# Score products on half the rows, the bias table loaded by each mixer, and a kernel's first two weight pairs in one sweep

## The chip, the cores and the metric

The kernel runs on one core of one Trainium2 chip. The metric is the time of one execution on the device, in microseconds (us), as the median of several runs. In the profile PE is the matrix engine (PEld its weight loads, which run beside the products), DVE the vector engine, ACT the scalar engine, POOL the general one, SP the engine that issues most transfers. Every engine works through its own list of instructions in order and waits on semaphores for the others.

## The reference

Two layers of a Conformer-like trunk on an input of 512 tokens by 1024 features, in fp32. Cut to what matters:

```python
for l in range(2):
    x = x + 0.5 * swiglu(rms_norm(x, ffn1_norm[l]), ...)       # 1024 -> 2816 -> 1024
    h = rms_norm(x, mix_norm[l])
    a, g, q, k, v = split(h @ w_in[l])                          # 512 columns each
    conv_out = conv_module(a, g, ...)                           # GLU, 31 causal taps, norm, swish
    # q, k: 4 heads x 2 maps x 64 features, each normed over its 64 features
    # v: 4 heads x 128 features; 128 queries at a time, causal
    s = q . k / sqrt(64) + bias[bucket(distance)]               # for each head and each of 2 maps
    p = softmax(s)
    attn = rms_norm((p[map 0] - lam * p[map 1]) @ v) * (1 - lambda_init)
    x = x + concat(conv_out, attn) @ w_out[l]
    x = x + 0.5 * swiglu(rms_norm(x, ffn2_norm[l]), ...)
```

The point for this study is the score: for each head there are two maps, and each contracts over 64 features only, whereas the array of PE has 128 rows.

## The kernel before, in words

Activations are kept with features on the partitions: `x` is 8 tiles of 128 features by 512 tokens. Every large fp32 product is made of three cheaper ones in a format that PE reads in one pass: an operand is split into a rounded part `hi` and a remainder `lo`, and `mm3` (L162, L165, L166) adds hi x hi, hi x lo and lo x hi. For a weight chunk of 128 by 1024, `chunk` (L104) issues the load on SP's queue, ACT makes `whi` (L96), DVE or POOL makes `wlo` (L97). The chunks live in rings of 5 raw, 4 `whi` and 4 `wlo` buffers, so a load waits until an older chunk has been used. An activation tile gets the same treatment in `Prep.tile`: ACT rounds `x` times the norm's gain into `acth` (L247), DVE makes `actl` (L248), ACT squares the tile (L252, L255) and POOL adds the squares. The root mean square of a token is only applied after the products: `rows_rstd` sums the squares over features with four PE transposes (L206) and DVE, `spread` puts the result on all partitions by two PE products (L230), and ACT copies it to `rb` (L234).

A feed-forward block has 22 pairs of a gate and an up chunk, in groups of 6, 8 and 8. The six of the first group are plain products with one PSUM bank for each of gate and up (three pairs of banks in rotation: pair 3 takes the banks of pair 0). The other 16 go through `seven` (L352), a seven-product scheme on half-size blocks. After the last pair of a group, its down products follow. For the very first block, the first pair's weight chunks are loaded ahead, in halves of four feature tiles (`lead`, `cuts=2`), between the first tile of `x` and the others. `first_products` multiplies pair 0 with feature tiles as the outer loop, gate and up as the inner one, and then pair 1, one bank after the other. The results are read by DVE with `rb` (L420, L422), gated, and split into `hh` and `hl` (L391, L392).

The mixer projects convolution inputs, keys, queries and values. The queries are transposed to features on the partitions (`to_features`, L598) and copied by ACT into `qz` (L605), which has a copy for each map; in the copy of map 0 the features of map 1 are zero, since the scale `gq` is zero there, and the reverse. So a score product contracts over all 128 rows, and the zeros take the other map out. A head's two score products (L677) are fp32 and go to one bank of tag `sc` and one of tag `po`; each is two PE instructions in the trace. DVE adds the bias table and takes the extreme value of a row (L681), ACT takes the exponential (L685), DVE combines both maps. `keys_first` transposes the combined map on PE (L698) and `values` multiplies it with the values (L707). `attend(n)` sets the scores of step n beside the transposes of step n-2 and the values of n-3, for 16 steps (4 blocks of queries, last one first, by 4 heads; the blocks have 512, 384, 256 and 128 keys). Beside this run the 31 taps of the convolution, on DVE, POOL and ACT (`conv_taps`), and the products of the value projection (L589 to L591) and, later, of the output projection (`ps_out`).

The bias table, 128 by 4 by 512, is made once: a small product with 33 rows (L459) looks up the buckets, two small DRAM tiles hold the result, and a load on POOL's queue with a skewed address pattern fills the tile `bias`, which stays in on-chip memory to the end. The parameter columns of layer 0 are loaded on ACT's queue, those of layer 1 on POOL's.

The order on each engine is fixed when the program is built: a scheduler simulates engines and queues with its own model and writes each engine's list. So a change of data flow can also change the order of products that the source does not touch. Ahead of the change's places, that order sets what can start when.

Of the kernel before, what the change touches and what calls it, by code (L numbers as in the profile page):

```python
# [11 lines left out]
F32 = mybir.dt.float32  # L12
# [3 lines left out]
ALU = mybir.AluOpType  # L16
# [50 lines left out]
def trunk(ctx: ExitStack, tc: tile.TileContext, xt, par, lamv, relb, onehot,  # L67
# [28 lines left out]
        S.activation(hi, raw, AF.Copy)  # L96
        (eng or V).tensor_tensor(out=lo, in0=raw, in1=f32(hi), op=ALU.subtract)  # L97

    def chunk(src, eng=None, cuts=1):
        raw, hi, lo = ring("wraw"), ring("whi"), ring("wlo")  # L100
        n = 1024 // cuts
        for c in range(cuts):
            s = slice(c * n, (c + 1) * n)
            nc.sync.dma_start(raw[:, s], src[:, s])  # L104
            parts_of(raw[:, s], hi[:, s], lo[:, s], eng)
        return hi, lo

    def gather(src, blocks, eng=None):
# [65 lines left out]
    for l in range(DEPTH):  # L174
        pt = const.tile([P, NPAR], F32, tag=f"par{l}", name=f"par{l}")
        pars.append(pt)
    nc.scalar.dma_start(pars[0], par[0])
    nc.sync.dma_start(x[:, 0, :], xt[0])
    lead = [chunk(gu1[0, 0, i], cuts=2) for i in range(2)]
    for k in range(1, KT):  # L180
        nc.sync.dma_start(x[:, k, :], xt[k])
    nc.gpsimd.dma_start(pars[1], par[1])
    ident = const.tile([P, P], F32, tag="ident", name="ident")
    make_identity(nc, ident)
    ones = const.tile([P, P], F32, tag="ones", name="ones")
# [75 lines left out]
    def wpart(w, b, n=P):  # L261
        return w[0][:, b * n : (b + 1) * n], w[1][:, b * n : (b + 1) * n]

    def products(pr, w, ps, i, pin=False):
        for k in range(KT):
            mm3(ps, wpart(w[i], k), pr[k], k == 0, k == KT - 1, pin=pin and k == 0)

    def first_products(pr, w, ps, early=False):

# [112 lines left out]
    def ffn(pr, gu, dn, after, lead=None, aside=None):  # L382
        with tc.tile_pool(name="ffn", bufs=1) as fp:
            r = halves = None
            for m0, many in PARTS:
                hh, held, late = [], [], []

                def gated(n, us):
                    hi = fp.tile([P, SEQ], F32R, tag=f"hh{n}", name="hh")
                    lo = fp.tile([P, SEQ], F32R, tag=f"hl{n}", name="hl")  # L390
                    S.activation(hi, us, AF.Copy)  # L391
                    V.tensor_tensor(lo, us, f32(hi), op=ALU.subtract)  # L392
                    hh.append((hi, lo))

                def finish():
                    if late:
                        n, rest = late.pop()
                        gated(n, rest())

                for mm in range(many):  # L400
                    m = m0 + mm
                    if m == 4 and aside:
                        aside()
                    if m >= PLAIN:
                        w = sums(gu[m, 0], gu[m, 1])
                        late.append((mm, seven(halves, w, pair_banks(m), fp, finish, mm == many - 1)))
                        continue
                    w = lead if lead and m == 0 else [chunk(gu[m, 0]), chunk(gu[m, 1])]
                    held.append((mm, w, pair_banks(m)))
                    if m == 0:  # L410
                        continue
                    if m == 1:
                        _, _, r = first_products(pr, [h[1] for h in held], [h[2] for h in held])
                    else:
                        for i in range(2):
                            products(pr, w, held[-1][2][i], i)
                    for n, _, ps in held:
                        gs = fp.tile([P, 2, SEQ], F32, tag="gn", name="gs", bufs=2)
                        us = gs[:, 1]
                        V.tensor_tensor(gs[:, 0], ps[0], r, op=ALU.mult)  # L420
                        S.activation(gs[:, 0], gs[:, 0], AF.Silu)
                        V.tensor_tensor(us, ps[1], r, op=ALU.mult)  # L422
                        V.tensor_tensor(us, us, gs[:, 0], op=ALU.mult)
                        gated(n, us)
                    held = []
                    if m == 1:
                        halves = Halves(fp, pr, r)
                finish()
                if m0 == 0:
                    halves.settle()  # L430
                blocks = [divmod(m0 + kk, HALF) for kk in range(many)]
                blocks = [(half, m * HALF + f) for m in range(KT) for half, f in blocks]
                w = None
                for m in range(KT):

                    ps = bank(turn_tag(m0 + many + m // 2), "ps_d")
                    for kk in range(many):
                        b = m * many + kk
                        if b % 8 == 0:
                            w = gather(dn, blocks[b : b + 8])  # L440
                        mm3(ps, wpart(w, b % 8), hh[kk], kk == 0, kk == many - 1)
                    V.scalar_tensor_tensor(x[:, m, :], ps, 0.5, x[:, m, :], op0=ALU.mult, op1=ALU.add)  # L442
                    if m0 + many == FT:
                        after(m)


    bias = const.tile([P, HEADS, SEQ], F32, tag="bias", name="bias")

    def make_bias():
        ext = small.tile([NBUCKET + 1, HEADS], F32, tag="relb", name="relb", bufs=1)  # L450
        V.memset(ext, MASK)
        nc.gpsimd.dma_start(ext[:NBUCKET, :], relb)
        d1 = dram.tile([HEADS, RLEN], F32, tag="d1", name="d1")
        for a, n in ((0, 512), (512, RLEN - 512)):
            oh = tmp.tile([P, SEQ], F32, tag="sq", name="oneh")[: NBUCKET + 1, :n]
            nc.gpsimd.dma_start(oh, onehot[:, a : a + n])
            row = tmp.tile([P, SEQ], F32, tag="sq", name="brow")[:HEADS, :n]
            ps = bank("tp", "ps_bias")
            T.matmul(ps[:HEADS, :n], ext, oh, start=True, stop=True)  # L459
            V.tensor_scalar(row, ps[:HEADS, :n], -1.0, None, op0=ALU.mult)  # L460
            nc.gpsimd.dma_start(d1[:, a : a + n], row)
        d2 = dram.tile([HEADS, P, RLEN], F32, tag="d2", name="d2")
        nc.gpsimd.dma_start(d2, d1.unsqueeze(1).broadcast_to([HEADS, P, RLEN]))
        skew = bass.AP(d2.tensor, d2.offset + P - 1, [[RLEN - 1, P], [P * RLEN, HEADS], [1, SEQ]])
        nc.gpsimd.dma_start(bias, skew)


    nlam, gq, gsub, ghalf = [], [], [], []
# [1 line left out]
    def make_scalars():  # L470
        for l in range(DEPTH):
# [9 lines left out]
            nl = const.tile([P, 1], F32, tag=f"nlam{l}", name=f"nlam{l}")  # L481
            V.scalar_tensor_tensor(nl, e[:, 1:2], -lambda_init(l), e[:, 0:1], op0=ALU.add, op1=ALU.subtract)
            nlam.append(nl)
            g = const.tile([P, 2], F32, tag=f"gq{l}", name=f"gq{l}")
            V.memset(g, 0.0)
            for m in range(2):
                d = slice(m * HD, (m + 1) * HD)
                V.scalar_tensor_tensor(
                    g[d, m : m + 1], col(l, "q_norm")[d], -math.sqrt(HD), col(l, "k_norm")[d],
                    op0=ALU.mult, op1=ALU.mult,  # L490
                )
# [12 lines left out]
    def mixer(l, pr, after):  # L504
        with tc.tile_pool(name="mix", bufs=1) as mp, tc.tile_pool(name="mt", bufs=2) as mt:
# [34 lines left out]

            qz = mp.tile([P, 2, HEADS, SEQ], F32, tag="qz", name="qz")
            kt = mp.tile([P, HEADS, SEQ], F32, tag="kt", name="kt")
            vv = mp.tile([P, NT, HEADS, VD], F32, tag="vv", name="vv")
            wts, qns = {}, {}
# [47 lines left out]
            def to_features(which, pair):  # L594
                for j in (2 * pair, 2 * pair + 1):
                    qn, pt = qns[which, j]
                    for h in range(HEADS):
                        T.transpose(pt[:, h * P : (h + 1) * P], qn[:, h * P : (h + 1) * P], ident)  # L598
                    pt = pt.rearrange("p (h t) -> p h t", h=HEADS)
                    t = slice(j * P, (j + 1) * P)  # L600
                    if which == 1:
                        S.activation(kt[:, :, t], pt, AF.Copy)
                    else:
                        for m in range(2):
                            S.activation(qz[:, m, :, t], pt, AF.Copy, scale=gq[l][:, m : m + 1])  # L605

            ch, cl = acth, actl

# [59 lines left out]
            def softmaxes(i, h):  # L668
# [5 lines left out]
                e0 = mt.tile([P, SEQ], F32, tag="e0", name="e", bufs=4)[:, :W]  # L674
                sm = sums[i]
                for m in range(2):
                    T.matmul(scs[m], qz[:, m, h, tq], kt[:, h, :W], start=True, stop=True)  # L677

                for m, (sc, e) in enumerate(zip(scs, (e0, scs[1]))):
                    mn = small.tile([P, 1], F32, tag=f"mn{m}", name="mn")  # L680
                    V.tensor_tensor_reduce(  # L681
                        out=e, in0=sc, in1=bias[:, h, SEQ - W :], scale=1.0, scalar=3e38,
                        op0=ALU.add, op1=ALU.min, accum_out=mn,
                    )
                    S.activation(e, e, AF.Exp, bias=mn, scale=-1.0, accum_out=sm[:, m, h : h + 1])  # L685
# [73 lines left out]
            to_features(0, 0)  # L759
            conv_in(CT - 1)  # L760
            to_features(0, 1)

            for n in range(2):
                attend(n)
# [127 lines left out]
```

## Time and profile before

| what | value |
|---|---|
| median of 3 runs | 1804.08 us (1803.64 to 1804.23) |
| profiled execution | 1805.29 us |
| its span in the trace | 1803.5 us |
| granted PE clock | 1.00 |
| PE busy | 1786.9 us |
| attention, layer 0 | 464.49 to 516.78 us |
| attention, layer 1 | 1356.90 to 1409.20 us |

A row of the timeline gives the start in us, the duration in us, engine, line, operation, output<-inputs, shape, how many were drawn together, and in brackets how long the engine had been idle and which engine's work ended that. Durations of PE's rows hold the pipeline's tail, so consecutive rows overlap; the spacing of starts is what a product costs. A row of the groups gives total busy us and the mean in ns after the bar. A row of the waits gives who waited for whom, then us in total, times, and the longest. A row of windows gives the stretch, its length, and the busy us of PE, PEld, DVE, ACT and POOL with counts, then the granted clock, the share of the DMA engines and GB/s.

### The profile page before, as it was taken

The numbers are of one execution on the slowest core, as the hardware profiler recorded it, in microseconds if no ns is written. First come the engines' busy times: TensorE is split into PE (matmuls) and PEld (weight loads), VectorE is DVE, ScalarE is ACT, GpSimd is POOL, SyncE is SP. The second block draws the span as 40 slices with busy tenths as digits, with TensorE's granted clock in tenths as the row PEclk, the third lists the DMA queues.
The fourth block names the chain that finished last, engine by engine and source line by source line (L and its number), as shares of the span: only waits on it lengthen the run. The fifth ranks groups of instructions, "written<-read, shape, count | busy, mean of one in ns | idle before, by whom it ended". The sixth has DMA issues, their size and how long they took to land.

```text
span 1803.5 us, 27857 instructions
## 1 busy us (share of the span) xinstructions
PE 1786.9 (99%) x10692; PEld 1584.1 (88%) x10692; DVE 1207.3 (67%) x1852; ACT 884.2 (49%) x1448; POOL 616.7 (34%) x432
## 2 busy tenths in 40 slices
PE   8999999999999999999999999999999999999999
PEld 6799899888778889899888998998887888998997
DVE  7857557568867857557576684665788587574662
ACT  5536346445854436346434462554558354463551
POOL 3035123269942024133110341322797320231320
PEclk9999999999999999999999999999999999999999
DMA  6357456322212347546433474653231133574561
GB/s 219 125 149 197 135 144 179 115 89 90 75 41 88 107 116 183 155 126 182 126 93 103 127 201 108 167 172 106 71 107 57 47 103 97 146 178 133 154 171 51
DMA packets 104853, 227.00 MB, mean 126 GB/s; under 512 B 11527, under 2 KB 29094, under 8 KB 104720
## 3 DMA queue, kind: packets, MB, share of 16 engines
q1 hardware_dynamic: 85536, 188.78, 32.3%
q0 software_dynamic: 19040, 36.36, 11.7%
q8 instruction: 83, 1.36, 0.3%
q14 instruction: 50, 0.41, 0.1%
q10 hardware_dynamic: 144, 0.08, 0.0%
HBM read 223.07 MB, written 3.42 MB: 126 GB/s over the span
## 4 chain that ended last, share of the span: by engine, by line
PE 95%; DVE 2%; ACT 1%; issue 1%; DMA 0%; SPq 0%; ACTq 0%; DVEq 0%
PE ps_pair L352 36%; PE ps_d L166 9%; PE ps_d L162 9%; PE ps_d L165 9%; PE ps_pair L166 6%; PE ps_pair L165 6%; PE ps_pair L162 6%; PE ps_pair L559 2%; PE ps_pair L560 2%; PE ps_pair L561 2%; PE ps_out L165 1%; PE ps_out L162 1%; PE ps_sc L677 1%; PE ps_out L166 1%; DVE actl L248 1%; PE ps_v L591 1%
## 5 line engine op out<-in xcount | busy, mean ns | idle before, releaser
L96 ACT ACTIVATE whi<-wraw 128x1024 fp32r<-128x1024 f32 (+1 forms) x578 | 459.0, 817 | 648.9 <-PE ps_d L165 226.1
L97 DVE TENSOR_TENSOR wlo<-wraw,whi 128x512 fp32r<-128x512 f32 (+1 forms) x534 | 513.6, 984 | 184.1 <-ACT whi L96 179.2
L352 PE MATMUL ps_pair<-acth,wlo 128*128 128x256 f32 x1024 | 289.8, 283 | 0.0
L352 PE MATMUL ps_pair<-actl,whi 128*128 128x256 f32 x1024 | 289.8, 283 | 0.0
L352 PE MATMUL ps_pair<-acth,whi 128*128 128x256 f32 x1024 | 289.7, 283 | 0.0
L165 PE MATMUL ps_d<-hl,whi 128*128 128x512 f32 x704 | 274.0, 389 | 0.0
L166 PE MATMUL ps_d<-hh,wlo 128*128 128x512 f32 x704 | 272.7, 389 | 0.0
L162 PE MATMUL ps_d<-hh,whi 128*128 128x512 f32 x704 | 268.9, 389 | 0.0
L140 POOL DMA_DIRECT2D wraw<-in_gu x64 | 77.2, 1207 | 452.6 <-DMA wraw<-in_gu 210.8
L352 PE MATMUL ps_pair<-th,wlo 128*128 128x256 f32 x768 | 217.3, 283 | 0.0
L352 PE MATMUL ps_pair<-tl,whi 128*128 128x256 f32 x768 | 217.2, 283 | 0.0
L352 PE MATMUL ps_pair<-th,whi 128*128 128x256 f32 x768 | 217.2, 283 | 0.0
L162 PE MATMUL ps_pair<-acth,whi 128*128 128x512 f32 x512 | 200.6, 395 | 5.5 <-ACT whi L96 5.5
L165 PE MATMUL ps_pair<-actl,whi 128*128 128x512 f32 x512 | 201.1, 393 | 2.0 <-DVE actl L248 1.6
L166 PE MATMUL ps_pair<-acth,wlo 128*128 128x512 f32 x512 | 200.5, 392 | 0.6 <-DVE wlo L97 0.6
L442 DVE SCALAR_TENSOR_TENSOR x<-ps_d,x 128x512 f32<-128x512 f32 x96 | 65.0, 689 | 197.3 <-PE ps_d L166 197.3
L352 PEld LDWEIGHTS ps_pair<-acth,whi 128*128 128x128 f32 x1024 | 196.6, 192 | 0.3
L352 PEld LDWEIGHTS ps_pair<-actl,whi 128*128 128x128 f32 x1024 | 196.6, 192 | 0.3
L352 PEld LDWEIGHTS ps_pair<-acth,wlo 128*128 128x128 f32 x1024 | 196.6, 192 | 0.0
L145 POOL TENSOR_TENSOR wraw<-wraw 128x512 f32<-128x512 f32 x64 | 87.8, 1373 | 304.3 <-DMA wraw<-in_gu 220.1
L165 PEld LDWEIGHTS ps_d<-hl,whi 128*128 128x128 f32 x704 | 132.2, 188 | 27.0
L166 PEld LDWEIGHTS ps_d<-hh,wlo 128*128 128x128 f32 x704 | 132.2, 188 | 27.0
(174 smaller groups left out, 3306.4 us busy)
## 6 DMA issues: line engine op xcount, KB each, us to landing
wraw<-in_gu SPq DMA_DIRECT2D x110, 512.0 KB, 3.6
wraw<-in_gu SPq DMA_DIRECT2D x196, 256.0 KB, 3.9
wraw<-in_gu POOLq DMA_DIRECT2D x64, 512.0 KB, 5.6
wraw<-in_wqkv SPq DMA_DIRECT2D x24, 512.0 KB, 3.5
wraw<-in_dn SPq DMA_DIRECT2D x52, 192.0 KB, 3.0
wraw<-in_wag SPq DMA_DIRECT2D x16, 512.0 KB, 3.5
wraw<-in_wout SPq DMA_DIRECT2D x16, 512.0 KB, 3.5
wraw<-in_dn SPq DMA_DIRECT2D x24, 320.0 KB, 3.4
```

The costliest lines, as they stand in the source:

```text
L96: S.activation(hi, raw, AF.Copy)
L97: (eng or V).tensor_tensor(out=lo, in0=raw, in1=f32(hi), op=ALU.subtract)
L140: nc.gpsimd.dma_start(two.rearrange("p (b c) -> p b c", b=2), u[:, h[0]].unsqueeze(1).broadcast_to([P, 2, 512]), accum_op=ALU.add)
L145: G.tensor_tensor(more[:, h[0]], two[:, h[1]], whole[:, h[0]], op=ALU.add)
L162: first = T.matmul(ps, wh, xh, start=start, stop=False)
L165: T.matmul(ps, wh, xl, start=False, stop=False)
L166: T.matmul(ps, wl, xh, start=False, stop=stop)
L352: mm = T.matmul(ps, l, r, start=first and i == j == 0, stop=False, skip_group_check=True)
L442: V.scalar_tensor_tensor(x[:, m, :], ps, 0.5, x[:, m, :], op0=ALU.mult, op1=ALU.add)
L559: T.matmul(ps[n], xh[:, t], wh, start=k == 0, stop=False)
L560: T.matmul(ps[n], xh[:, t], wl, start=False, stop=False)
L561: T.matmul(ps[n], xl[:, t], wh, start=False, stop=k == KT - 1)
```

## The change

Three things change.

First, the start. All four weight chunks of pairs 0 and 1 are loaded by halves: the first feature tile of `x`, the first halves of all four chunks, three tiles of `x`, the fifth tile, the second halves, the last three tiles. A new function `lead_products` takes pair 0 and pair 1 in one sweep, with feature tiles outermost and the four banks inside, and only then sums the squares' rows and spreads them. The parameters of both layers are loaded on ACT's queue.

Second, the bias table. `make_bias` ends with the address pattern `skew`; each mixer allocates its own `bias` tile in its own pool and loads it on SP's queue. In the built program that load stands behind the second of a layer's loads of key weights.

Third, the scores. The queries are kept once (`qt`, one ACT copy with a scale `gq` of one column), and a map's score product takes 64 partitions of `qt` and `kt`, the lower half for map 0 and the upper for map 1. In the built program these products are placed on the array as tiles of 64 rows by 128 columns, at row 0 or row 64. The scheduler writes another order for the score products: in each layer the 32 stand in 19 groups between other products, where before they stood in 22.

```diff
-    nc.scalar.dma_start(pars[0], par[0])
-    nc.sync.dma_start(x[:, 0, :], xt[0])
-    lead = [chunk(gu1[0, 0, i], cuts=2) for i in range(2)]
-    for k in range(1, KT):
-        nc.sync.dma_start(x[:, k, :], xt[k])
-    nc.gpsimd.dma_start(pars[1], par[1])
+    for l in range(DEPTH):
+        nc.scalar.dma_start(pars[l], par[l])
+
+    lead = [[ring("wraw"), ring("whi"), ring("wlo")] for _ in range(4)]
+    for half in range(2):
+        h, kk = slice(half * 512, (half + 1) * 512), range(half * KT // 2, (half + 1) * KT // 2)
+        nc.sync.dma_start(x[:, kk[0], :], xt[kk[0]])
+        for n, (raw, hi, lo) in enumerate(lead):
+            nc.sync.dma_start(raw[:, h], gu1[0, n // 2, n % 2][:, h])
+            parts_of(raw[:, h], hi[:, h], lo[:, h])
+        for k in kk[1:]:
+            nc.sync.dma_start(x[:, k, :], xt[k])
+    lead = [[tuple(t[1:]) for t in lead[2 * m : 2 * m + 2]] for m in range(2)]
...
+    def lead_products(pr, w, ps):
+
+        for k in range(KT):
+            for n in range(2):
+                for i in range(2):
+                    mm3(ps[n][i], wpart(w[n][i], k), pr[k], k == 0, k == KT - 1)
+        rc, v = rows_rstd(pr.s, DM)
+        return rc, v, spread(rc, "rb", split=True)
...
-                    w = lead if lead and m == 0 else [chunk(gu[m, 0]), chunk(gu[m, 1])]
+                    w = lead[m] if lead and m < 2 else [chunk(gu[m, 0]), chunk(gu[m, 1])]
...
-                        _, _, r = first_products(pr, [h[1] for h in held], [h[2] for h in held])
+                        first = lead_products if lead else first_products
+                        _, _, r = first(pr, [h[1] for h in held], [h[2] for h in held])
...
-    bias = const.tile([P, HEADS, SEQ], F32, tag="bias", name="bias")
+    skew = []
...
-        nc.gpsimd.dma_start(bias, skew)
...
-            qz = mp.tile([P, 2, HEADS, SEQ], F32, tag="qz", name="qz")
+            qt = mp.tile([P, HEADS, SEQ], F32, tag="qt", name="qt")
...
-                        for m in range(2):
-                            S.activation(qz[:, m, :, t], pt, AF.Copy, scale=gq[l][:, m : m + 1])
+                        S.activation(qt[:, :, t], pt, AF.Copy, scale=gq[l])
...
                 for m in range(2):
-                    T.matmul(scs[m], qz[:, m, h, tq], kt[:, h, :W], start=True, stop=True)
+                    half = slice(m * HD, (m + 1) * HD)
+                    T.matmul(scs[m], qt[half, h, tq], kt[half, h, :W], start=True, stop=True)
...
+            bias = mp.tile([P, HEADS, SEQ], F32, tag="bias", name="bias")
+            nc.sync.dma_start(bias, skew[0])
+            row["bias"] = bias
```

More of the change, by code (lines that the diff above doesn't have):

```diff
@@ L97, in parts_of, with chunk @@
         (eng or V).tensor_tensor(out=lo, in0=raw, in1=f32(hi), op=ALU.subtract)
-    def chunk(src, eng=None, cuts=1):
+    def chunk(src, eng=None):
         raw, hi, lo = ring("wraw"), ring("whi"), ring("wlo")
[L101 to L105, printed above, removed]
+        nc.sync.dma_start(raw, src)
+        parts_of(raw, hi, lo, eng)
         return hi, lo
@@ L463, in make_bias @@
         nc.gpsimd.dma_start(d2, d1.unsqueeze(1).broadcast_to([HEADS, P, RLEN]))
-        skew = bass.AP(d2.tensor, d2.offset + P - 1, [[RLEN - 1, P], [P * RLEN, HEADS], [1, SEQ]])
-        nc.gpsimd.dma_start(bias, skew)
+        skew.append(bass.AP(d2.tensor, d2.offset + P - 1, [[RLEN - 1, P], [P * RLEN, HEADS], [1, SEQ]]))
     nlam, gq, gsub, ghalf = [], [], [], []
@@ L483, in make_scalars @@
             nlam.append(nl)
-            g = const.tile([P, 2], F32, tag=f"gq{l}", name=f"gq{l}")
-            V.memset(g, 0.0)
-            for m in range(2):
[L487 to L491, printed above, removed]
+            g = const.tile([P, 1], F32, tag=f"gq{l}", name=f"gq{l}")
+            V.scalar_tensor_tensor(g, col(l, "q_norm"), -math.sqrt(HD), col(l, "k_norm"), op0=ALU.mult, op1=ALU.mult)
             gq.append(g)
@@ L603, in to_features @@
                     else:
-                        for m in range(2):
-                            S.activation(qz[:, m, :, t], pt, AF.Copy, scale=gq[l][:, m : m + 1])
+                        S.activation(qt[:, :, t], pt, AF.Copy, scale=gq[l])
             ch, cl = acth, actl
@@ L681, in softmaxes @@
                     V.tensor_tensor_reduce(
-                        out=e, in0=sc, in1=bias[:, h, SEQ - W :], scale=1.0, scalar=3e38,
+                        out=e, in0=sc, in1=row["bias"][:, h, SEQ - W :], scale=1.0, scalar=3e38,
                         op0=ALU.add, op1=ALU.min, accum_out=mn,
```

## The prediction

> **What bounds the kernel now.** I read the page first (engine shares, then the chain that ended last), then PE's waits, then PE's timeline in the two places that the diff touches.
>
> ```profile
> span 1803.5 us, 27857 instructions
> PE 1786.9 (99%) x10692; PEld 1584.1 (88%) x10692; DVE 1207.3 (67%) x1852; ACT 884.2 (49%) x1448; POOL 616.7 (34%) x432
> PE 95%; DVE 2%; ACT 1%; issue 1%; DMA 0%; SPq 0%; ACTq 0%; DVEq 0%
> ```
>
> ```profile
> PE ps_pair L162 <- ACT whi L96: 5.5, 1, 5.5
> PE ps_out L162 <- ACT acth L661: 2.5, 2, 1.3
> ```
>
> PE (matmul) is busy 1786.9 of 1803.5 us and makes 95% of the chain, so time moves only if PE has less to do or waits less. The profiled execution took 1805.29 us: 1.79 around its span of 1803.5, and 1.21 above the median of 1804.08. I work out shifts against the profiled execution and apply them to the median. 0.2% of it is 3.6 us, about what a measurement can tell from no change.
>
> Two stages can move: the first 50 us, and the attention of each layer (464.49 to 516.78, and 1356.90 to 1409.20).
>
> ```profile
> 5.53 0.80 PE L162 MATMUL ps_pair<-acth,whi 128*128 128x512 f32 x1 [5.53 <-ACT whi L96]
> 12.21 0.63 PE L166 MATMUL ps_pair<-acth,wlo 128*128 128x512 f32 x1
> 12.63 0.63 PE L165 MATMUL ps_pair<-actl,whi 128*128 128x512 f32 x1
> 24.00 0.50 PE L166 MATMUL ps_pair<-acth,wlo 128*128 128x512 f32 x1 [0.58 <-DVE wlo L97]
> 24.33 0.40 PE L162 MATMUL ps_pair<-acth,whi 128*128 128x512 f32 x1
> 46.44 0.39 PE L162 MATMUL ps_pair<-acth,whi 128*128 128x512 f32 x1
> ```
>
> PE starts at 5.53. Its first dozen products stand 0.42 apart (12.21, 12.63). The row at 24.00 is the 51st PE instruction, 46.44 the 149th, which opens pair 3, whose bank was pair 0's: 22.44 / 98 = 0.229 apiece, full pace (0.227 where only products stand). So what the start can gain was lost before 24.
>
> **The change part by part.**
>
> *Start, the gain.* Four half chunks load before x1, in place of two. The second half chunk now lands at about 8.0, and the third and fourth behind it:
>
> ```profile
> 8.04 1.88 ACT L96 ACTIVATE whi<-wraw 128x512 fp32r<-128x512 f32 x3 [2.56 <-DMA wraw<-in_gu]
> 10.62 0.62 ACT L255 ACTIVATE sq<-x 128x512 f32<-128x512 f32 x1
> 11.14 0.71 ACT L247 ACTIVATE acth<-x,par 128x512 fp32r<-128x512 f32 x1
> ```
>
> PE's first products still start at 5.5, then wait for that chunk until about 8.7. The 12 products of feature tile 0 end at about 13.0, at the slow spacing as now. From there 12 products follow per feature tile, 2.7 us of PE (12 x 0.227), while ACT needs at most 1.33 us for a tile's square and rounding (0.62 + 0.71). PE no longer waits for x: 84 x 0.227 = 19.1, so the 96th product is issued at about 32.1; four row sums to 32.55; 46 products of pair 2 put the 145th instruction at 43.0 and the 149th, nominally, at 43.9. Against 46.44 this gains 2.5 us. The parameter load that moves from POOL's queue to ACT's costs ACT one issue before x has landed; DVE gets those columns no later than PE's weights. I take nothing, with bounds of half a us to either side, the size of one small instruction there.
>
> *Start, the price.* The statistics now come behind all 96 products; the spread stands at instructions 146 and 148, right ahead of pair 3, where before it had 47 products behind it. Pair 3's bank must first be read through rb, and the instruction order puts two roundings between:
>
> ```profile
> 28.68 0.39 PE L165 MATMUL ps_pair<-actl,whi 128*128 128x512 f32 x1
> 29.11 1.06 ACT L96 ACTIVATE whi<-wraw 128x1024 fp32r<-128x1024 f32 x1 [4.81 <-PE ps_pair L165]
> 35.05 1.06 ACT L96 ACTIVATE whi<-wraw 128x1024 fp32r<-128x1024 f32 x1 [4.88 <-PE ps_pair L165]
> 36.15 1.23 DVE L97 TENSOR_TENSOR wlo<-wraw,whi 128x1024 fp32r<-128x1024 f32 x1 [1.91 <-ACT whi L96]
> 39.16 0.60 ACT L234 ACTIVATE rb<-ps_spread 128x512 f32<-128x512 f32 x1 [3.04 <-PE ps_spread L230]
> 39.79 0.69 DVE L420 TENSOR_TENSOR gs<-ps_pair,rb 128x512 f32<-128x512 f32 x1
> ```
>
> ACT's last whi before the rb copy takes the buffer whose last reader is instruction 145. From that: 0.43 to ACT's start (28.68 to 29.11), 1.10 to DVE's wlo (35.05 to 36.15), 1.23 for it, 0.69 for the first gs: 3.45 us. The rb copy (0.60) fits inside this. Pair 3 nominally follows instruction 145 by 0.91, so PE stands still 2.54 us and instruction 149 comes at 46.45. The start as a whole: 0.0. Bounds: -2.5 if the stall is hidden; +1.9 if PE goes back to 0.42 spacing after standing (some 10 products by 0.19). The longest wait of PE behind the start is the 1.3 of the waits above, so 2.54 is untested; I take no slowing, as after that one.
>
> What else is late: DVE runs some 3 us later against PE. Its next deadline is far:
>
> ```profile
> 86.69 0.69 DVE L392 TENSOR_TENSOR hl<-gs,hh 128x512 fp32r<-128x512 f32 x1 [0.70 <-ACT hh L391]
> 93.03 0.39 PE L165 MATMUL ps_d<-hl,whi 128*128 128x512 f32 x1
> 93.68 0.69 DVE L442 SCALAR_TENSOR_TENSOR x<-ps_d,x 128x512 f32<-128x512 f32 x1 [6.29 <-PE ps_d L166]
> ```
>
> The last hl ends at 87.4 and is needed at 93.03: 5.7 us of slack, and DVE then idles 6.29. Cost nothing; without that slack, up to 3.
>
> *Bias.* The table's one load on POOL's queue goes; each mixer loads it on SP's, behind the second of the loads of the wqkv weights, after a wait for PE to leave the region.
>
> ```profile
> bias<-d POOLq DMA_DIRECT2D x1, 1024.0 KB, 6.5
> 353.25 23.04 SPq L104 DMA_DIRECT2D wraw<-in_wqkv  x5
> SPq L104 <- POOL wlo L97: 303.5, 42, 36.4
> 465.58 2.74 PE L677 MATMUL ps_sc<-kt,qz 128*128 128x512 f32 x6
> ```
>
> One MB more, 6.5 us; its first reader follows the scores at 465.58, about 100 us after its place on the queue (five wqkv loads are issued from 353.25 on, spread over 23 us because they wait for ring slots, up to 36.4 us a time). The load and what stands behind it have slack. POOL loses one issue, with nobody waiting. Cost 0; up to +3 a layer (half of 6.5) if it holds weights that PE waits for.
>
> *Queries once.* Eight ACT copies a layer become four.
>
> ```profile
> L605 ACT ACTIVATE qz<-ps_pair,gq 128x512 f32<-128x512 f32 x16 | 9.7, 689 | 6.2 <-PE ps_pair L598 6.2
> ```
>
> Eight fewer at about 0.6: 4.8 us of ACT in all, where PE is full (52.00 of 52.00 from 440 to 492, below). Worth 0. The small memsets and the second scaling of gq that go lie at the start, where DVE waits for loads: 0.
>
> *Scores by row halves.* 128 PE instructions (two to an fp32 product), 64 a layer. Each now uses 64 of the 128 rows, on rows 0 to 63 for map 0, 64 to 127 for map 1.
>
> ```profile
> L677 PE MATMUL ps_sc<-kt,qz 128*128 128x512 f32 x32 | 15.0, 592 | 0.0
> L677 PE MATMUL ps_sc<-kt,qz 128*128 128x384 f32 x32 | 12.3, 487 | 0.0
> L677 PE MATMUL ps_sc<-kt,qz 128*128 128x256 f32 x32 | 9.3, 382 | 0.0
> L677 PE MATMUL ps_sc<-kt,qz 128*128 128x128 f32 x32 | 6.2, 285 | 0.0
> 57.09 0.39 PE L166 MATMUL ps_pair<-acth,wlo 128*128 128x512 f32 x1
> 57.41 1.02 PE L459 MATMUL ps_bias<-oneh,relb 33*4 33x512 f32 x2
> 58.36 0.50 PE L162 MATMUL ps_pair<-acth,whi 128*128 128x512 f32 x1
> 58.69 0.39 PE L165 MATMUL ps_pair<-actl,whi 128*128 128x512 f32 x1
> ```
>
> The means hold the pipeline's tail; a 512-wide instruction takes 0.43 of PE (six of them in 2.74 less the tail), narrower ones in proportion: 0.32, 0.21, 0.11. That is 16 x (0.43+0.32+0.21+0.11) = 17.1 us a layer. If two halves could always run at once, half of it, 8.6, would go. But the order that the scheduler writes for the changed kernel has the 32 scores of a layer in 19 groups between other products, and most hold one half only. If an instruction can begin beside the one before it when that is of the other half, and starts stay in order, then the order saves at most 2.6 us a layer (1.3 of it in the first group of four 512-wide scores).
>
> Against it stands a change of array shape at both ends of each group. The only work of fewer rows in the trace before is L459 with 33: from 57.09 to 58.69 are 1.60 us, where the two full products take 0.227 each and the two instructions 0.86, so 0.28 is the price of going there and back. Nineteen groups cost 19 x 0.28 = 5.3 us a layer; the other bound is 0, as for today's full-height scores (465.58 to the next products loses nothing). I take 0.28, as it is the row of the same kind.
>
> The Trainium skill, page "TensorEngine Tiling (Array Packing)", section "Tiling Modes", says that changing the tiling mode, not just the tile, drains TensorE; the 0.28 agrees with it, and nothing in the trace before shows two tiles at once. By the page's twofold speedup for 64-row tiles, with no drain, the time would be some 12 us under mine, 1793; that lies in the second rival below and in its chance.
>
> Where PE's time is not the whole end of this stage, waits absorb some:
>
> ```profile
> 464.49:516.78 52.29, 50.03 (x263) 37.36 (x261) 45.47 (x144) 45.08 (x112) 37.35 (x30) 1.00 0.13 41
> 440.00:492.00 52.00, 52.00 (x242) 40.27 (x241) 42.86 (x88) 39.29 (x73) 50.28 (x31) 1.00 0.28 90
> 490.00:500.00 10.00, 9.36 (x65) 7.83 (x64) 9.45 (x34) 7.71 (x24) 5.52 (x6) 1.00 0.10 40
> 508.11 0.50 PE L162 MATMUL ps_out<-acth,whi 128*128 128x512 f32 x1 [1.27 <-ACT acth L661]
> ```
>
> Columns are window, length, then PE, PEld, DVE, ACT, POOL. PE idles 2.26 of 52.29 there, late, where DVE (9.45 of 10) and the convolution set the pace: at 508.11 PE waits for its result. So of 5.3 - 2.6 = +2.7 a layer, some 2.3 is absorbed: +0.4, twice +0.8. With the start at 0.0 and the bias at 0: 1805.29 + 0.8 = 1806.1 for the profiled execution, 1804.9 for the median.
>
> **The rivals.**
>
> *The halves' drains decide (slower).* Place: the 19 groups of each layer. If no neighbours overlap, +5.3 a layer; if besides nothing is absorbed because the extra falls before the convolution's results, both layers cost +10.6, giving 1814.7; with the overlap but no absorption +5.4, giving 1809.5. It decides as soon as drains exceed overlap and absorption (2.6 + 2.3 a layer) by 1.8, a price of 0.35 a group. For: the 0.28, and PE 52.00 of 52.00 up to 492. Against: 33 rows by 4 columns is another shape than 64 by 128.
>
> *The overlap wins (faster).* Free changes of shape: -2.6 a layer, up to -4 if earlier softmaxes pull the DVE chain; with the start's -2.5 at best, 1804.1 - 5.2 to 1804.1 - 10.5: 1793.6 to 1798.9, middle 1797. For: full-height scores change at no cost; against: DVE and convolution bound the last 25 us, and absorb a PE that is early.
>
> *The start alone.* Stall hidden: -2.5, 1802.4. PE slow again after the stall: +1.9, 1806.8. The skill's page "TensorE: Matmul & The Clock Gate", Part 1, has the clock fall when about 3.4 us hold little work; the 2.54 us here are under that, and the trace shows no such wait.
>
> *The bias load holds up weights.* Up to +6: 1810.9. Against: over 100 us between load and reader.
>
> **How the numbers follow.** Forecast (small terms cancel, 1801 to 1807.7): 0.43. Drains decide: 0.28. Overlap wins: 0.22. Bias: 0.03. The start alone, 0.04, falls inside 0.2% in either case. So within 0.2%: 0.46 (0.42 of the first after its edges, 0.04); slower by over 0.2%: 0.31; faster: 0.23. The likeliest case's own range is 1801.0 to 1807.7; the range that leaves out 2 in 10 reaches into both sides, 1797.5 to 1811.
>
> **What would show it.** In the changed kernel's trace: PE's wait near 6.3 to 8.7, no waits of PE for L97 or L248 up to 32, a stall of about 2.5 us ahead of pair 3 near 44 released by DVE's gs, pair 3 at 46.4; scores of 64 rows, neighbours of the other half starting closer than 0.43, and 0.28 beyond the products' own time at each group; the last projection's first products at the same distance from 464.5 as before. The prediction is wrong if pair 3 opens at 44, if neighbours' starts fall together everywhere, or if the attention's 52.3 us change by over 2.

## The result and the profile after

The changed kernel takes 1807.82 us (median of 20 runs, 1806.35 to 1808.53) against 1804.31 for the kernel before (20 runs, 1803.64 to 1807.03): a ratio of 1.0017, 95% interval 1.0011 to 1.0023. It is slower by 0.17%: the interval lies clear of no difference at all, and the median inside the 0.2% that the forecast called no change (the interval reaches past that edge); 1804.9 was predicted. The profiled execution took 1807.83.

The page after (span, engine shares), and PE's waits (us in total, times, longest):

```profile
span 1806.1 us, 27855 instructions
PE 1791.1 (99%) x10692; PEld 1581.8 (88%) x10692; DVE 1214.0 (67%) x1850; ACT 879.2 (49%) x1442; POOL 626.0 (35%) x430
...
PE ps_pair L159 <- ACT whi L96: 6.0, 1, 6.0
PE ps_pair L159 <- DVE gs L434: 2.5, 1, 2.5
PE ps_o L714 <- ACT at L707: 1.4, 2, 0.7
```

PE is busy 4.2 us longer, part of it at half clock, as shown below. The two waits for the convolution's `acth` (2.5 us in all before) are gone, and a single wait of 2.5 us, for the first gating read `gs`, is new.

Three matching instructions on the timeline of each kernel say where the time went: the first residual add behind the second group of the first feed-forward block, and the last residual add of each mixer. First before, then after:

```profile
208.35 0.69 DVE L442 SCALAR_TENSOR_TENSOR x<-ps_d,x 128x512 f32<-128x512 f32 x1 [5.13 <-PE ps_d L166]
563.44 0.41 DVE L785 TENSOR_TENSOR x<-ps_out,x 128x256 f32<-128x256 f32 x1
1455.86 0.41 DVE L785 TENSOR_TENSOR x<-ps_out,x 128x256 f32<-128x256 f32 x1
```

```profile
208.68 0.69 DVE L456 SCALAR_TENSOR_TENSOR x<-ps_d,x 128x512 f32<-128x512 f32 x1 [5.15 <-PE ps_d L163]
565.05 0.41 DVE L795 TENSOR_TENSOR x<-ps_out,x 128x256 f32<-128x256 f32 x1
1458.74 0.41 DVE L795 TENSOR_TENSOR x<-ps_out,x 128x256 f32<-128x256 f32 x1
```

The differences are +0.33, +1.61 and +2.88: the start loses 0.33, each mixer 1.28 and 1.27, and nothing happens between them. The last residual add of the kernel is 2.90 late as well (1799.56 and 1802.46); the span is longer by 2.6 only, since the last store ends 0.3 sooner behind it. These are one execution of each kernel, and that of the kernel before, 1805.29, lies 1.0 over its median; so the 2.9 is less than the 3.5 between the medians, and the start's 0.33 is uncertain by about 1 (the parts run alone, below, bear on it).

The start, on PE's timeline after and by its windows (window, length, busy us of PE, PEld, DVE, ACT, POOL; then the granted clock):

```profile
5.97 0.80 PE L159 MATMUL ps_pair<-acth,whi 128*128 128x512 f32 x1 [5.97 <-ACT whi L96]
6.56 0.63 PE L162 MATMUL ps_pair<-actl,whi 128*128 128x512 f32 x1
...
45.02 0.50 PE L159 MATMUL ps_pair<-acth,whi 128*128 128x512 f32 x1 [2.51 <-DVE gs L434]
...
46.25 0.63 PE L162 MATMUL ps_pair<-actl,whi 128*128 128x512 f32 x1
46.68 0.63 PE L163 MATMUL ps_pair<-acth,wlo 128*128 128x512 f32 x1
```

```profile
42.36:45.77 3.41, 0.90 (x4) 0.67 (x4) 3.19 (x7) 3.03 (x5) 0.54 (x1) 1.00 0.26 57
45.77:49.18 3.41, 3.41 (x9) 2.65 (x8) 3.41 (x6) 0.63 (x1) 0.00 (x0) 0.50 0.46 142
49.18:52.59 3.41, 3.41 (x16) 2.79 (x15) 3.41 (x9) 0.37 (x1) 0.00 (x0) 1.00 0.00 0
```

Pair 3 opens at 45.02, 1.42 us earlier than before (46.44), although PE stood for 2.51 us ahead of it. Then PE's clock is granted at one half for exactly 3.41 us, in which products stand 0.43 apart (46.25, 46.68). At half pace 3.41 us of work loses about 1.7: -1.42 + 1.7 = +0.3, the difference found at 208. In 15 of the 20 executions the mean clock over the span is 0.999, and their times lie at 1807.50 to 1808.53; the five with 1.000 lie at 1806.35 to 1806.91. A mean of 0.999 alone would not tell, since some executions of the kernel before show it too, at no longer time; its profile has the clock fall at 1801.83, behind the last product. Here the times part with it, so I take the fall at pair 3 to happen in most executions, not in all.

The attention, on PE's timeline after: the first group of scores, four products of 512 keys, and its neighbours:

```profile
462.53 0.39 PE L596 MATMUL ps_v<-whi,acth 128*128 128x512 f32 x1
462.85 1.99 PE L684 MATMUL ps_sc<-kt,qt 64*128 64x512 f32 x8
464.76 0.50 PE L597 MATMUL ps_v<-wlo,acth 128*128 128x512 f32 x1
...
466.94 0.39 PE L598 MATMUL ps_v<-whi,actl 128*128 128x512 f32 x1
467.25 1.98 PE L684 MATMUL ps_sc<-kt,qt 64*128 64x512 f32 x4
469.17 0.50 PE L596 MATMUL ps_v<-whi,acth 128*128 128x512 f32 x1
```

From 462.53 to 464.76 are 2.23 us; 0.227 is the product ahead, so the group takes 2.0 where eight instructions one after the other would take 8 x 0.43 = 3.44. At 467.25 four instructions of one half alone take 2.0 as well (469.17 less 466.94, where the product ahead starts, less 0.227), 0.28 over 4 x 0.43. In the first group the eight instructions start in pairs, at 462.85, 463.38, 463.81 and 464.24, the two of a pair 0.01 apart. Both readings fit one rule: the halves run beside each other, each in its own order, and a group costs 0.28 for going there and back. Done so for all groups of layer 0 (start of the product behind, less start and spacing of the product ahead), the scores take 18.50 us before, waits inside the groups included, and 19.52 after.

### The profile page after: what moved, and what is told of

It is laid out like the page before. It is cut to its first block, busy times and chain, and to the rows that moved or that the text cites. A ratio compares the mean times of both kernels' runs of the same rounds, so it can differ in the third digit from the quotient of the medians.

```text
span 1806.1 us, 27855 instructions
## 1 busy us (share of the span) xinstructions
PE 1791.1 (99%) x10692; PEld 1581.8 (88%) x10692; DVE 1214.0 (67%) x1850; ACT 879.2 (49%) x1442; POOL 626.0 (35%) x430
## 3 DMA queue, kind: packets, MB, share of 16 engines
HBM read 224.12 MB, written 3.42 MB: 126 GB/s over the span
## 5 line engine op out<-in xcount | busy, mean ns | idle before, releaser
L96 ACT ACTIVATE whi<-wraw 128x512 fp32r<-128x512 f32 (+1 forms) x580 | 458.1, 813 | 663.0 <-PE ps_d L162 227.4
L97 DVE TENSOR_TENSOR wlo<-wraw,whi 128x512 fp32r<-128x512 f32 (+1 forms) x536 | 523.0, 998 | 182.5 <-ACT whi L96 177.5
L159 PEld LDWEIGHTS ps_d<-hh,whi 128*128 128x128 f32 x704 | 132.3, 188 | 27.0
```

Of the source, the lines that this page charges most:

```text
L159: first = T.matmul(ps, wh, xh, start=start, stop=False)
```

## The experiments

My account of this result was: 0.3 us (or -1.2 without the fall of the clock) from the start, 1.3 a layer from the scores (19 groups x 0.29 = 5.5 of drains, less 3.8 of overlap), nothing from the bias table. Rivals: the bias load behind SP's queue is what the mixers lost; the start is the whole of it; the overlap is small; what is late in the start only moves. The kernel before, run beside them, took 1804.62 (beside the first four runs), 1804.49 (the next four) and 1804.62 (the last three).

**Each part alone.** In `start_only` the scores and the bias table are as before; `bias_only` has only

```diff
+            bias = mp.tile([P, HEADS, SEQ], F32, tag="bias", name="bias")
+            nc.sync.dma_start(bias, skew[0])
```

with `skew` in place of the one load, and `scores_only` has only `qt`, `gq` of one column, and

```diff
-                    T.matmul(scs[m], qz[:, m, h, tq], kt[:, h, :W], start=True, stop=True)
+                    half = slice(m * HD, (m + 1) * HD)
+                    T.matmul(scs[m], qt[half, h, tq], kt[half, h, :W], start=True, stop=True)
```

> Only the new start, scores and bias table as before. Theory (each part has its own price): the wait of 2.5 us ahead of pair 3 and the slow products behind it are there as in the changed kernel; the time is 0.3 us above before where the PE clock falls after that wait, about 1.2 below where it does not: 1803.1 to 1804.6 against 1804.3. Rival (the start is the whole loss): about 1807.5.

> Only the bias table moved to each mixer's load on SP's queue. Theory: hidden, 1804.3 with at most 0.4 to either side. Rival (the load holds weights behind it, and that is the 1.3 us a layer that the mixers lost): 1806.8.

> Only the queries kept once and the score products on 64 rows; start and bias as before. Theory (19 drains of 0.29 us a layer, 5.5, less 3.8 of overlap between the halves, not much absorbed): 1.3 us a layer, so 1806.8. Rival (the bias load made the mixers slower): 1804.3.

Measured: `start_only` 1805.95 (ratio 1.0007, 0.9998 to 1.0015), `bias_only` 1804.46 (0.9999, 0.9990 to 1.0008), `scores_only` 1807.00 (1.0012, 1.0003 to 1.0021). The bias load costs nothing that can be measured, and its rival falls. The three matching instructions of `scores_only` on its timeline:

```profile
208.13 0.69 DVE L442 SCALAR_TENSOR_TENSOR x<-ps_d,x 128x512 f32<-128x512 f32 x1 [5.15 <-PE ps_d L166]
564.48 0.41 DVE L779 TENSOR_TENSOR x<-ps_out,x 128x256 f32<-128x256 f32 x1
1458.15 0.41 DVE L779 TENSOR_TENSOR x<-ps_out,x 128x256 f32<-128x256 f32 x1
```

Against before they stand at -0.22, +1.04 and +2.29: 1.26 and 1.25 a layer, as in the changed kernel. So the scores alone make the mixers' loss. `start_only` came out 1.3 above the kernel before, by its median, over the 0.3 that I gave; its interval holds both. By medians the parts make +1.3, -0.2 and +2.4, together 3.5, which is the whole difference; so the start's share is nearer 1.3 than the 0.33 of the one pair of profiles. The profiles show how far the start differs between executions. With the old start, the first of the three rows stands at 208.35, 207.74, 208.13 and 208.22 (`before`, `bias_only`, `scores_only`, `first_two`). With the new one it stands at 207.60 and 207.55 where the clock does not fall (`start_only` and `one_half`, below), and at 208.68 and 209.54 where it does (the changed kernel and `pairs`, below).

The profiled execution of `start_only`, at 1804.53 the fastest of its eleven, had the same wait and no fall of the clock:

```profile
45.55 0.50 PE L159 MATMUL ps_pair<-acth,whi 128*128 128x512 f32 x1 [2.51 <-DVE gs L434]
...
41.42:44.83 3.41, 1.62 (x8) 0.98 (x6) 1.72 (x5) 2.44 (x4) 0.54 (x1) 1.00 0.37 114
44.83:48.25 3.42, 2.70 (x12) 2.25 (x13) 3.42 (x7) 1.74 (x3) 0.00 (x0) 1.00 0.67 170
```

These windows are laid at whole multiples of 3.413 us from where the clock first rose in that execution. Here the wait (43.04 to 45.55) straddles a boundary, and PE is busy 1.62 and 2.70 us of the two; in the changed kernel's profile it fell inside one, and PE was busy 0.90. The same 2.51 us wait comes in two more profiles. In `pairs` it lies inside a window, PE is busy 0.90, and the clock falls; in `one_half` it straddles a boundary, PE is busy 2.19 and 2.14 of the two windows, and the clock does not fall. In the kept traces, all falls ahead of the last product come a whole number of such windows after the first rise: 10 in the changed kernel, 10, 147 and 410 in `pairs`, 146 and 409 in `spread_mid_pairs`. That the position against this grid decides for the 2.51 us wait is what these four executions suggest; no run moved it on purpose. It need not lie inside a window whole: if the grid's position were even, that would be so in 0.90 / 3.41, about a quarter of the executions, and 15 of 20 fell.

**Both maps on the same half.** `one_half` takes the overlap away and leaves the drains and every engine's order:

```diff
-                    half = slice(m * HD, (m + 1) * HD)
+                    half = slice(0, HD)
```

> The changed kernel with both maps' score products on rows 0 to 63 (map 1 reads map 0's features, so its scores are left out); every engine's order stays the same. No two neighbours can run beside each other any more, the drains stay. Theory (the overlap is worth 3.8 us of PE a layer, and little of it lies under waits): 5 to 7.6 us above the changed kernel's 1807.8, that is 1813 to 1815.4. Rival (starts stay in order, so that the overlap is at most 2.6 a layer, and mostly under waits): 1808 to 1811.

Measured: 1813.69, 5.9 above the changed kernel (ratio to before 1.0051, 1.0038 to 1.0063). The first group on its timeline:

```profile
461.41 0.39 PE L596 MATMUL ps_v<-whi,acth 128*128 128x512 f32 x1
461.73 3.70 PE L684 MATMUL ps_sc<-kt,qt 64*128 64x512 f32 x8
465.35 0.50 PE L597 MATMUL ps_v<-wlo,acth 128*128 128x512 f32 x1
```

It takes 3.71 us (465.35 - 461.41 - 0.227) in place of 2.0: 8 x 0.43 and 0.27. All groups of layer 0 take 23.10 us, 3.6 more than in the changed kernel. That is the overlap's whole worth, 3.6 us a layer where I had counted 2.6 at most, and it reaches the end: its matching instructions lie at 207.55, 567.40 and 1464.61, that is 4.76 and 4.79 us a layer over before, 3.5 over the changed kernel. Both layers make 7.0; by the medians it is 5.9, and by the profiles the start takes 1.1 off the 7.0 (207.55 against 208.68), since the clock did not fall there.

**The wait ahead of pair 3.** `spread_mid` issues the spread inside pair 2's products, pinned there, and gates pairs 0 to 2 after that:

```diff
...
+                    if m == 1 and lead:
+                        rc = lead_products(pr, [h[1] for h in held], [h[2] for h in held])
+                        continue
+                    if m == 2 and lead:
+                        for i in range(2):
+                            for k in range(KT):
+                                at = i == 1 and k == 2
+                                if at:
+                                    r = spread(rc, "rb", split=True, pin=True)
+                                mm3(held[-1][2][i], wpart(w[i], k), pr[k], k == 0, k == KT - 1, pin=at)
...
```

`lo_pool` only shortens the wait:

```diff
-                    w = lead[m] if lead and m < 2 else [chunk(gu[m, 0]), chunk(gu[m, 1])]
+                    w = lead[m] if lead and m < 2 else [chunk(gu[m, 0]), chunk(gu[m, 1], G if lead and m == 4 else None)]
```

> The changed kernel with the spread of the row factors pinned into the last quarter-to-half of pair 2's products instead of right behind them, so that rb and the first gating reads of pair 0's bank come before pair 3 needs it. Theory (the wait of 2.5 us and the fall of the PE clock behind it cost 2.5 + 1.5): 4 us below the changed kernel where the clock fell, 1803.8, and no row of the start at 0.43 us spacing behind pair 3. Rival (the work that is late only moves, DVE being the bound of the start): 1806 or more, with a wait of PE elsewhere before 115 us.

> The changed kernel with one remainder (wlo of pair 4's up chunk) made on POOL instead of DVE, which takes 1.23 us of DVE from the chain ahead of the first gating read. Theory (the chain sets the wait; the scalar engine's rb copy is next): the wait ahead of pair 3 shrinks from 2.5 to about 1.8 us. Whether PE's clock still falls is what this run tells: if the fall needs the longer wait, pair 3 runs at 0.23 and the time is 1805.6 (0.7 + 1.5 less); if any wait of 1.8 does it, 1807.1.

Measured: `spread_mid` 1803.97 (0.9998, 0.9989 to 1.0007) and `lo_pool` 1805.46 (1.0006, 0.9997 to 1.0015), 3.9 and 2.4 below the changed kernel, where 4.0 and 2.2 were expected. In `spread_mid` there is no wait ahead of pair 3, which opens at 44.14. In `lo_pool`, the opening of pair 3 and the window that holds the wait:

```profile
44.12 0.50 PE L159 MATMUL ps_pair<-acth,whi 128*128 128x512 f32 x1 [1.65 <-DVE gs L434]
44.46 0.40 PE L162 MATMUL ps_pair<-actl,whi 128*128 128x512 f32 x1
44.70 0.39 PE L163 MATMUL ps_pair<-acth,wlo 128*128 128x512 f32 x1
...
42.30:45.71 3.41, 1.76 (x8) 1.33 (x8) 2.98 (x7) 3.38 (x6) 2.53 (x2) 1.00 0.24 59
```

The wait is 1.65, whole inside a window, and products go on at 0.23; in all eleven executions the mean clock is 1.000. So the chain of roundings does set the wait, and the shorter wait does not bring the clock down.

**A head's two products side by side.** `pairs` forces what the scheduler does not do, and `spread_mid_pairs` adds `spread_mid` to it:

```diff
-                for m in range(2):
+                for m in (1, 0):
                     half = slice(m * HD, (m + 1) * HD)
-                    T.matmul(scs[m], qt[half, h, tq], kt[half, h, :W], start=True, stop=True)
+                    mm = T.matmul(scs[m], qt[half, h, tq], kt[half, h, :W], start=True, stop=True)
+                    if m == 0:
+                        tc.keep_in_program_order(mm)
```

> The changed kernel with a head's two score products issued side by side (map 1 first, map 0 pinned behind it): 13 groups a layer in place of 19, each with both halves. Theory: drains 13 x 0.29 = 3.8, scores 8.6 in place of 17.2, so PE's work falls from 18.9 to 12.4 a layer; if half of that reaches the end, 3.2 a layer, 1801.4; all of it 1794.8. Rival (the vector engine and the convolution bound the attention): no gain, 1806 to 1809, PE waiting longer for the convolution's results.

> Both edits together (spread in the middle of pair 2, score products side by side). Theory: the two gains add, since they lie in different stages: the sum of what each alone gives against the changed kernel.

Measured: 1815.89 (1.0064, 1.0051 to 1.0077) and 1813.19 (1.0049, 1.0036 to 1.0062). My theory fell. The rival was nearer, but its 1806 to 1809 was missed as well, and it put the loss in the wrong place: PE does not wait for the convolution. The two effects do about add, as expected: +8.1 and -3.9 on the changed kernel make 1812.0. PE's waits in `pairs`, and its windows at the end of layer 0's attention:

```profile
PE ps_at L707 <- ACT at L709: 6.6, 6, 1.5
PE ps_sc L684 <- DVE e L700: 6.3, 9, 1.6
PE ps_o L743 <- DVE ov L731: 3.4, 4, 1.3
PE ps_v L596 <- ACT vv L599: 2.8, 2, 1.4
```

```profile
510.89:514.31 3.42, 1.80 (x15) 1.26 (x15) 3.31 (x11) 2.83 (x9) 1.68 (x2) 1.00 0.00 0
514.31:521.13 6.82, 5.74 (x21) 4.38 (x20) 6.25 (x24) 4.98 (x16) 2.23 (x2) 0.50 0.01 2
```

The saving in PE's work is there: without the waits inside them, layer 0's 13 groups take about 13.6 us, where 12.4 was expected and the changed kernel's 19 groups take 19.2. But each group of two products waits for both banks, and PE waits some 19 us in the two layers for DVE and ACT. That the softmax of a step starts later for it is my reading, not a run's. Then it comes worse: after a stretch of 3.42 us in which PE was busy 1.80 (1.78 in layer 1), between several short waits, the clock falls to one half for 6.82 us in each layer. Busy time alone does not say when it falls: 1.76 in `lo_pool` and 1.62 in `start_only` were less, and it did not fall. What sets these windows apart is open. In `pairs` it falls at pair 3 too; in `spread_mid_pairs` only in the attention.

**Only the first two steps.** `first_two` is the kernel before, with 64-row products, side by side, for the first two steps of a layer alone; `start_mid` is the new start with the spread in pair 2 and nothing else; the third has both.

```diff
-                for m in range(2):
-                    T.matmul(scs[m], qz[:, m, h, tq], kt[:, h, :W], start=True, stop=True)
+                early = (i, h) in steps[:2]
+                for m in (1, 0) if early else (0, 1):
+                    half = slice(m * HD, (m + 1) * HD) if early else slice(0, P)
+                    mm = T.matmul(scs[m], qz[half, m, h, tq], kt[half, h, :W], start=True, stop=True)
+                    if early and m == 0:
+                        tc.keep_in_program_order(mm)
```

> The kernel before (start, bias, zero-padded queries as before) with 64-row score products only for the first two steps of each layer, four products side by side in one group among the value products, all later scores on 128 rows. Theory (0.29 for a group's drains, less the overlap): that group takes 2.0 us of PE where 3.4 stood, and it lies where PE never waits: 1.4 us less a layer, 1801.6 against 1804.5. Rival (an earlier softmax gives nothing because the vector engine and the convolution set the end of the attention): 1804.5, with PE waiting 1.4 us longer before the convolution's results.

> Only the new start, with the spread pinned into pair 2; scores and bias as before. Theory: pair 3 opens about 2.4 us earlier than in the kernel before, no wait ahead of it, no slow products: 1802.1. Rival (what is late only moves): 1804.5.

> Both edits of this call together. Theory: they lie in different stages and add, 2.4 + 2.8: 1799.3, under both kernels. Rival: whatever of the two fails alone is missing here as well.

Measured: `first_two` 1803.73 (0.9997, 0.9988 to 1.0006), `start_mid` 1801.82 (0.9984, 0.9975 to 0.9993), `start_mid_first_two` 1800.85 (0.9981, 0.9972 to 0.9990). The start gives 2.8, where 2.4 was expected, and the last kernel is under both. The first two steps give 0.9 in place of 2.8, and the interval of `first_two` takes in no gain at all; the 0.8 on its timeline (0.4 a layer) and the 1.0 that they give on top of `start_mid` agree with 0.9. On the timeline of `first_two`, the group and two waits of PE further on, and behind them the wait of the kernel before:

```profile
464.66 1.99 PE L679 MATMUL ps_sc<-kt,qz 64*128 64x512 f32 x8
466.57 0.50 PE L589 MATMUL ps_v<-whi,acth 128*128 128x512 f32 x1
...
490.80 1.16 PE L711 MATMUL ps_o<-vv,at 128*128 128x128 f32 x8 [0.37 <-ACT at L704]
494.23 0.55 PE L702 MATMUL ps_at<-ident,e 128*128 128x128 f32 x3 [0.65 <-ACT at L704]
```

```profile
494.78 0.55 PE L698 MATMUL ps_at<-ident,e 128*128 128x128 f32 x3 [0.44 <-ACT at L700]
```

The group takes 2.0 as in the changed kernel, so PE is 1.4 us ahead; before 495 PE then waits longer for transposed maps than in the kernel before (0.37 and 0.65 here, 0.44 there), and its later instructions stand about 0.4 a layer ahead of before. Most of what PE gains in a stage that it fills is eaten by the waits for the softmax behind it.

## Why the prediction was right, and where not

The forecast of no change above 0.2% held, but only just: +0.8 us was forecast and +3.5 measured, with the edge at 3.6, and 1807.82 lies 0.1 above the 1807.7 that the forecast names. That it held is in part luck, since errors to both sides cancelled. In the sum's own terms, on the two profiles, the start was to be -2.5 + 2.5 = 0.0 and is -3.9 + 2.5 + 1.7 = +0.3; a layer was to be 5.3 - 2.6 - 2.3 = +0.4 and is 5.5 - 3.6 - 0.6 = +1.3. Two terms failed to the slow side: the clock's fall, put at nothing, and the absorbed waits. With the clock's fall, one rival (PE slow again after the stall) came true beside the forecast.

*Start, the gain.* Undersized in this execution, and in part by chance. PE did not wait for the second chunk between 6.3 and 8.7: its products follow each other from 5.97 at the slow pace, and the clock rose at 11.64, about 1.4 us earlier than I had it. Pair 3 opens at 45.02, not 46.45. But neither is fixed by the change. In `pairs`, whose first 146 products are the same in the same order, PE does wait:

```profile
7.60 0.79 PE L159 MATMUL ps_pair<-acth,whi 128*128 128x512 f32 x1 [0.65 <-ACT whi L96]
```

There the clock rose at 12.55 and pair 3 opened at 45.92. In the kept profiles the rise comes 6.3 to 9.1 us after PE's first product with the old start. With the new one it comes 4.1 to 5.7 us after it in the five where PE does not wait for that chunk, and 4.9 to 7.5 us after it in the four where it does.

*Start, the price.* Right: 2.54 predicted from five rows, 2.51 measured, and released by `gs` as named. `lo_pool` and `spread_mid` confirm the chain. The count was off by two, without effect on the times: pair 3 opens with PE's 151st instruction, behind the two of the spread, the 148th and the 150th.

*No slowing after the wait.* Wrong, and the one step that I took against an end of its own range (+1.9 a bound, about 1.7 measured). I took the 1.3 us wait of the trace as the nearest case, and held that 2.54 stays under the 3.4 us of the clock's rule. The Trainium skill, page "TensorE: Matmul & The Clock Gate", Part 1, describes windows of 3.4 us that run free of the kernel. The falls at whole numbers of 3.413 us behind the first rise, and that rise at 4.1 to 9.1 us behind PE's first product, agree with it. I read the length and passed over that a wait shorter than a window can fill most of one. The profile has 0.90 us of work in the window ahead of the fall, and in `pairs` 1.80: a window need not be empty. How full it may be is open, since 1.76 and 1.62 did not bring the clock down elsewhere.

*Bias.* Right: nothing.

*Queries once.* Nothing of it shows apart from the scores; I did not test it alone.

*Drains.* Right: 0.28 from a product of 33 rows, 0.28 to 0.31 for groups of 64 rows; 19 groups make 5.5 against 5.3.

*Overlap.* Undersized, 3.6 in place of 2.6 at most. I had starts in order over both halves; the trace has the first instructions of both halves start together, and each half go on in its own order.

*Absorbed waits.* Wrong: 2.3 a layer was to be absorbed. 5.5 - 3.6 = 1.9 of extra work, and 1.26 to 1.28 came out, so some 0.6 was absorbed. PE's idle time between 440 and 540 us falls only from 2.26 to 1.28. The waits for the convolution (1.4) did go, but waits of 0.71 for transposed maps and 0.28 for DVE are among those that took their place. That the extra work also delays the softmaxes that PE later waits for is my explanation; no run tested it by itself. In `one_half` PE still idles 1.16 a layer, so its 3.6 of extra work came through to the end almost whole (3.5).

*The signs named.* The last projection's first product does not stand at the same distance: it comes 48.1 us behind the first score product (462.85 to 510.91), and before it was 43.6 (464.49 to 508.11). The scheduler's order had moved both, so this distance says little on the time; the 1.28 between the residual adds does.

*Two figures.* The middle of the second rival's 1793.6 to 1798.9 is 1796, not 1797. The 12 us for a twofold speed are not worked out there: half of 17.1 a layer, less the 2.3 of waits, would be 12.6 in all.

## What to carry to other kernels

Price a change of array shape per group and count the groups in the order that the scheduler writes: here 0.28 us a group ate what running two halves at once gave, and forcing fewer groups cost more in waits than it saved. Idle time of a bound engine inside a chain of dependent steps is not simply slack: here 1.9 us of added work a layer cost 1.3, and of 1.4 saved early in a layer 0.4 was left. And count a wait of the matrix engine against the clock: 2.5 us of waiting brought 1.7 us more in most executions, so moving one small step earlier gained 3.9 us, more than the whole change had cost.

## What the runs showed that I had not expected

The clock falls for whole steps of 3.41 us (one in the start, two in the attention of `pairs`), at whole steps from its first rise, and whether a 2.51 us wait makes it fall differs from execution to execution of one kernel. Products on the two row halves run beside each other: their first instructions start 0.01 us apart, and four products in one group take 2.0 us in place of 3.7.
